# FFN gate and up as seven block products instead of eight in a two-layer hybrid decoder, one core

## The chip, the cores and the metric

The kernel runs on one core of a Trainium2 chip. The metric is the device time of one execution in microseconds (us). TensorE (PE) multiplies, with its weight loads shown apart as PEld; VectorE (DVE) and ScalarE (ACT) do elementwise work; GpSimd (POOL) does the inverse square roots; SyncE (SP) issues the DMAs.

## What is computed

Two layers over 1040 tokens (16 meta tokens and 1024 others), model width 1024, FFN width 2816. Cut to what matters here:

```python
h = h + concat(attn_out, conv_out) @ w_out[l]
hn = rmsnorm(h, norm2_g[l])
gate, up = split(hn @ w_gate_up[l], 2)
h = h + (silu(gate) * up) @ w_down[l]
```

The attention and convolution halves ahead of it, the other norm and the rotary tables are as before in both kernels.

## The kernel before

Activations lie transposed: 128 channels on the partitions, tokens along the free axis, eight such blocks (`acc[n]`) for the residual. Every float32 factor of a matmul is split into a float32r part `hi` (ACT copy) and a rest `lo` (DVE subtraction), and a product is the three passes hi·hi, hi·lo, lo·hi: `mm3` (L248 to L255) with one weight load for each matmul of 128x128 weights by a chunk of tokens. `wsplit` (L195 to L215) loads a weight block in two halves of at most 128x512 into `wr`, and makes `wh` on ACT (L209) and `wl` on DVE (L210). `fetch` (L240) makes a weight one place ahead of its use.

Layer 0 goes over tokens in chunks of 272, 384 and 384 (`CH0`), layer 1 in two of 512 (`CH1`), since the meta tokens are not needed at its end. After attention and convolution come, in each layer:

- the second half of the output projection ("oc", L737 to L748): eight blocks n of 12 matmuls for each chunk, into the `pj` banks of PSUM (three of them); DVE adds each chunk to `acc[n]` (L268), `gsplit` (L263) makes `hh[n]`, `hl[n]` (the FFN's input with the norm's gain), and `accum_sq` (L140) sums the squares;
- `rsqrt_bcast` (L157): sums over partitions by PE, the power on POOL, and a broadcast by 16 or 18 small matmuls with `ones` (L186);
- the FFN (L753 to L804): for each of the 22 blocks j of 128 FFN channels and each chunk, 24 matmuls for gate and 24 for up (contraction 8 x 128, three passes), then DVE and ACT make silu(gate)·up and split it into `mh`, `ml`. After each of four groups (6, 6, 5, 5 blocks in layer 0; 6, 6, 6, 4 in layer 1) the down projection runs: eight blocks n, each chunk 3·(blocks in the group) matmuls, added to `acc[n]`. In the last group each chunk is also split again for the next layer (layer 0) or normed and stored (layer 1, in chunks of 512, 256, 256), and its squares are summed.

The order on each engine is made by the framework's scheduler from the order of the code; each engine works through its own list in order. PSUM has eight banks: `pj` 3, `sc` 3, `tr` 2; the FFN turns through all eight (`PS_ORDER`).

Of the kernel before, what the change touches and what calls it, by code (L numbers as in the profile page):

```python
# [10 lines left out]
F32 = mybir.dt.float32  # L11
# [3 lines left out]
ALU = mybir.AluOpType  # L15
# [15 lines left out]
GROUPS = ((6, 6, 5, 5), (6, 6, 6, 4))  # L31
# [8 lines left out]
WB = 3  # L40
# [5 lines left out]
RB = 4  # L46
SB = 15
PS_BUFS = {"pj": 3, "sc": 3, "tr": 2}
PS_ORDER = ("pj", "tr", "pj", "tr", "pj", "sc", "sc", "sc")
# [4 lines left out]
# columns of the packed per-partition parameters  # L54
# [28 lines left out]
def build(tc, xT, w_in, w_out, w_gu, w_down, params, lams, ctab, consts, tabs, outT):  # L83
# [31 lines left out]
    def tmp(dt=F32):  # L115
        return tp.tile([P, 512], dt, tag="T", name=nm("T"), bufs=TB)
# [40 lines left out]
    def rsqrt_bcast(sq, n, blocks=range(NQ), out=None, cols=False):  # L157
        """[128, tokens] sums over partitions -> (sum/n + eps)^-1/2 on every partition."""
# [36 lines left out]
    def wsplit(src, kn, scale=None, where=None):  # L195
        """Load [128, kn, 128] of weights and split it (scaled) into float32r parts."""
        if where is None:
            hi = wp.tile([P, KD * P], F32R, tag="wh", name=nm("wh"), bufs=WB)
            lo = wp.tile([P, KD * P], F32R, tag="wl", name=nm("wl"), bufs=WB)
        else:  # L200
            hi, lo = where[:, :kn * P], where[:, kn * P:2 * kn * P]
        hk = -(-kn // 2)
        for b0, b1 in ((0, hk), (hk, kn)):
            raw = wp.tile([P, 4 * P], F32, tag="wr", name=nm("wr"), bufs=RB)
            rw = raw[:, :(b1 - b0) * P]
            nc.sync.dma_start(rw, src[:, b0:b1, :].rearrange("p k n -> p (k n)"))
            sl = slice(b0 * P, b1 * P)
            if scale is None:
                S.activation(hi[:, sl], rw, AF.Copy)  # L209
                V.tensor_tensor(lo[:, sl], rw, hi[:, sl].bitcast(F32), op=ALU.subtract)  # L210
            else:
                S.activation(hi[:, sl], rw, AF.Copy, scale=scale)
                V.scalar_tensor_tensor(lo[:, sl], rw, scale, hi[:, sl].bitcast(F32),
                                       op0=ALU.mult, op1=ALU.subtract)
        return hi, lo  # L215

    # Weights in the order of their use; each fetch also prepares the next one.
    plan, made = [], {}

    def make_plan(sub_ts):  # L220
        for l in range(DEPTH):
# [4 lines left out]
            for n in range(KD):  # L226
                plan.append((("oc", l, n), (w_out[l, n, :, 4:8, :], 4), False))
            f0 = 0
            for gi, gn in enumerate(GROUPS[l]):
                for j in range(f0, f0 + gn):  # L230
                    for t in range(2):
                        plan.append((("gu", l, j, t), (w_gu[l, j, t], KD), False))
# [7 lines left out]
    def fetch(*key):  # L240
        i = [p[0] for p in plan].index(key)
        while made_n[0] < len(plan) and made_n[0] <= i + AHEAD:
            k, args, own = plan[made_n[0]]
            made[k] = wsplit(*args, where=big(F32R) if own else None)
            made_n[0] += 1
        return made.pop(key)

    def mm3(out, w, xs, c0, c1):  # L248
        """out = sum over k of w[k]^T x[k], each factor in its two float32r parts."""
        wh, wl = w  # L250
        n = len(xs)
        for q, (wt, xi) in enumerate(((wh, 0), (wh, 1), (wl, 0))):
            for k in range(n):
                T_.matmul(out, lhsT=wt[:, k * P:(k + 1) * P], rhs=xs[k][xi][:, c0:c1],  # L254
# [52 lines left out]
    def project_qk(l, h, cosr, sinr, st, pre=None):  # L307
# [3 lines left out]
        else:  # L311
# [85 lines left out]
    def attention(l, h, stacks, v0, vv, nlam, cats, fin):  # L397
        q0 = 1 if l == DEPTH - 1 else 0
        oall = big()
        o0 = tp.tile([META, P], F32, tag="o0", name=nm("o0"), bufs=2)  # L400
# [5 lines left out]
        def scores(i):  # L406
# [3 lines left out]
            for c in range(2):  # L410
# [3 lines left out]
                for k0, k1 in key_chunks(qb):  # L414
# [5 lines left out]
                    if e > k0:  # L420
                        # the maximum of each part lands next to the diagonal block
# [15 lines left out]
        def turn(i, a):  # L437
# [4 lines left out]
            for g, ge in gs:  # L442
                ptg = ps("tr")
                if g == 1:
                    T_.transpose(ptg[:META, 384:384 + sz], a[:sz, 0:META], ident[:sz, :sz])
                    aT0 = tp.tile([META, P], F32, tag="aT0", name=nm("aT0"), bufs=2)
# [4 lines left out]
                aT = tp.tile([P, 512], F32, tag="aT", name=nm("aT"), bufs=3)  # L451
# [63 lines left out]
    def glu(l, j, rs, out):  # L515
        z = big()
        ct = None
        if j not in DVEJ:
            ct = tp.tile([P, 320], F32, tag="ct", name=nm("ct"), bufs=2)
# [26 lines left out]
    def conv_dve(l, j, z, out):  # L546
        """Queue the taps of one channel block as background work on VectorE."""
# [10 lines left out]
    def conv(l, j, z, ct, out):  # L558
# [9 lines left out]
        for g in range(8):  # L568
            w = wp.tile([P, 5 * P], F32, tag="cw", name=nm("cw"), bufs=CB)
# [72 lines left out]
    for l in range(DEPTH):  # L642
        last = l == DEPTH - 1
# [91 lines left out]
        drain(fill)  # L735
        sqacc = big()
        for n in range(KD):  # L737
            w = fetch("oc", l, n)
            for c0, c1 in chunks:
                po = ps("pj")  # L740
                mm3(po[:, :c1 - c0], w, ccats, c0, c1)
                t = acc[n]
                tt(t[:, c0:c1], po[:, :c1 - c0], t[:, c0:c1], ALU.add)
                if n == KD - 1:
                    accum_sq(sqacc, n == 0, t[:, c0:c1], c0, c1)
                gsplit(hh[n][:, c0:c1], hl[n][:, c0:c1], t[:, c0:c1], col("g2", l, n))
                if n < KD - 1:
                    accum_sq(sqacc, n == 0, t[:, c0:c1], c0, c1)  # L748

# [1 line left out]
        rs = rsqrt_bcast(sqacc, D, range(1 if last else 0, NQ))  # L751
        nps[0] = 0
        f0 = 0  # L753
        for gi, gn in enumerate(GROUPS[l]):
            mids = []
            for j in range(f0, f0 + gn):
                wg = fetch("gu", l, j, 0)
                wu = fetch("gu", l, j, 1)
                mh, ml = big(F32R), big(F32R)
                for c0, c1 in chunks:  # L760
                    n = c1 - c0
                    pg, pu = ps("any"), ps("any")
                    mm3(pg[:, :n], wg, hs, c0, c1)
                    mm3(pu[:, :n], wu, hs, c0, c1)
                    t1, t2 = tmp(), tmp()
                    tt(t1[:, :n], pg[:, :n], rs[:, c0:c1], ALU.mult)
                    S.activation(t1[:, :n], t1[:, :n], AF.Silu)  # L767
                    tt(t2[:, :n], pu[:, :n], rs[:, c0:c1], ALU.mult)
                    tt(t2[:, :n], t2[:, :n], t1[:, :n], ALU.mult)
                    split(mh[:, c0:c1], ml[:, c0:c1], t2[:, :n])  # L770
                mids.append((mh, ml))
            end = gi == len(GROUPS[l]) - 1
            if end:
                sqacc = big()
            ws = {}
            if end and last:
                order = [(n, [c]) for c in CHF for n in range(KD)]
                rs = big()
            else:
                order = [(n, chunks) for n in range(KD)]  # L780
            for n, cs in order:
# [4 lines left out]
                for c0, c1 in cs:  # L786
                    po = ps("any")
# [109 lines left out]
```

## Time and profile before

| | |
|---|---|
| median of 3 runs | 2504.01 us (2503.77 to 2506.76) |
| profiled execution, span | 2505.8 us (its time outside the span is not listed apart) |
| PE busy | 2464.8 us (98%), 14140 matmuls |
| PEld busy | 2253.5 us (90%) |
| DVE busy | 1321.0 us (53%) |
| ACT busy | 823.0 us (33%) |
| granted TensorE clock, mean | 0.995 |

A busy PE says that matmuls follow each other, each overlapping the next; how fast they follow is read from the pieces of the chain of waits: its length divided by the count of matmuls in it. "x24" is such a count. In a timeline, "x2" joins instructions that overlap by a little, so the time from one start to the next is shorter than the duration of one.

### The profile page before, as it was taken

What the parts mean: (1) busy time and instruction counts of PE and PEld (TensorE: products, weight loads), DVE (VectorE), ACT (ScalarE), POOL (GpSimd) and SP (SyncE); (2) the same over time, 40 slices, a digit from 0 to 9 for tenths busy, and PEclk for the clock granted to TensorE, in tenths of its full rate; (3) what the DMA queues carried; (4) which work ended last, traced back from release to release, by engine and by line L of the source; (5) the groups of instructions that cost most, each with busy time, mean ns of one, the idle gap of its engine ahead of it and who ended that gap; (6) DMA issues with size and microseconds to landing.
All of it is one profiled execution on the core that took longest, in us unless ns stands there. A gap on an engine that the chain in (4) does not pass through costs nothing.

```text
span 2505.8 us, 35578 instructions
## 1 busy us (share of the span) xinstructions
PE 2464.8 (98%) x14140; PEld 2253.5 (90%) x14140; DVE 1321.0 (53%) x2967; ACT 823.0 (33%) x1816; POOL 31.8 (1%) x21
## 2 busy tenths in 40 slices
PE   7999999999999999999999999999999999999998
PEld 7999999999999999999999999977888888888887
DVE  7676899743333323333556668987333333333336
ACT  5555543622112112112435555436211121121112
POOL 0000000000000000000000000000000000000000
PEclk9999999999999999999999999999999999999999
DMA  4431322111111111111244303221111111111112
GB/s 165 118 77 39 107 60 53 55 50 38 47 57 43 39 55 48 37 59 37 92 121 101 73 30 111 62 49 60 43 45 50 56 41 47 51 49 44 53 33 84
DMA packets 91365, 155.21 MB, mean 62 GB/s; under 512 B 10816, under 2 KB 46656, under 8 KB 91200
## 3 DMA queue, kind: packets, MB, share of 16 engines
q1 hardware_dynamic: 91200, 152.95, 20.8%
q8 instruction: 111, 1.82, 0.3%
q14 instruction: 54, 0.44, 0.1%
HBM read 114.64 MB, written 8.45 MB: 49 GB/s over the span
## 4 chain that ended last, share of the span: by engine, by line
PE 89%; DVE 7%; issue 1%; POOL 1%; ACT 1%; DMA 1%; SPq 0%; POOLq 0%; DVEq 0%; ACTq 0%
PE pj L254 41%; PE sc L254 22%; PE tr L254 15%; PE tr L465 4%; DVE S L552 3%; PE sc L417 1%; PE tr L454 1%; PE sc L418 1%; PE sc L186 1%; DVE S L268 1%; POOL s L174 1%; PE sc L579 1%; PE sc L167 0%; PE sc L598 0%; POOL s L497 0%
## 5 line engine op out<-in xcount | busy, mean ns | idle before, releaser
L209 ACT ACTIVATE wh<-wr 128x512 fp32r<-128x512 f32 (+2 forms) x406 | 213.8, 570 | 504.6 <-PE sc L254 203.3
L254 PE MATMUL pj<-hh,wh 128*128 128x384 f32 (+2 forms) x1552 | 316.2, 339 | 0.7 <-ACT S L330 0.7
L254 PE MATMUL pj<-hl,wh 128*128 128x384 f32 (+2 forms) x1552 | 310.8, 337 | 0.0
L254 PE MATMUL pj<-hh,wl 128*128 128x384 f32 (+2 forms) x1552 | 307.4, 336 | 0.0
L254 PEld LDWEIGHTS pj<-hl,wh 128*128 128x128 f32 x1552 | 259.1, 188 | 12.8 <-issue 0.2
L254 PEld LDWEIGHTS pj<-hh,wl 128*128 128x128 f32 x1552 | 258.5, 189 | 12.8 <-issue 0.2
L254 PEld LDWEIGHTS pj<-hh,wh 128*128 128x128 f32 x1552 | 257.4, 189 | 14.0 <-ACT S L330 1.0
L254 PE MATMUL pj<-S,wh 128*128 128x384 f32 (+2 forms) x1252 | 261.4, 351 | 2.8 <-ACT S L260 1.3
L210 DVE TENSOR_TENSOR wl<-wr,wh 128x512 fp32r<-128x512 f32 (+2 forms) x406 | 239.2, 616 | 10.1 <-ACT wh L209 8.7
L254 PEld LDWEIGHTS pj<-S,wh 128*128 128x128 f32 x1252 | 214.4, 188 | 25.4 <-ACT S L260 2.3
L268 DVE TENSOR_TENSOR T<-pj,S 128x384 f32<-128x384 f32 (+2 forms) x185 | 99.2, 546 | 213.6 <-PE pj L254 208.7
L260 ACT ACTIVATE S<-T 128x384 fp32r<-128x384 f32 (+2 forms) x110 | 60.4, 549 | 393.0 <-DVE T L268 393.0
L268 DVE TENSOR_TENSOR T<-sc,S 128x512 f32<-128x512 f32 (+2 forms) x81 | 47.6, 588 | 240.4 <-PE sc L254 240.4
L552 DVE SCALAR_TENSOR_TENSOR S<-S,par,S 128x1039 f32<-128x1039 f32 (+14 forms) x120 | 153.4, 1278 | 0.5
L767 ACT ACTIVATE T<-T 128x384 f32<-128x384 f32 (+2 forms) x110 | 60.4, 549 | 254.4 <-DVE T L268 254.4
L268 DVE TENSOR_TENSOR T<-tr,S 128x384 f32<-128x384 f32 (+2 forms) x62 | 35.7, 580 | 198.7 <-PE tr L254 198.7
L254 PE MATMUL pj<-S,wl 128*128 128x384 f32 (+2 forms) x626 | 139.1, 349 | 0.0
L254 PE MATMUL sc<-hh,wl 128*128 128x512 f32 (+2 forms) x648 | 134.9, 351 | 0.0
L254 PE MATMUL sc<-hh,wh 128*128 128x512 f32 (+2 forms) x648 | 134.9, 351 | 0.0
L254 PE MATMUL sc<-hl,wh 128*128 128x512 f32 (+2 forms) x648 | 134.7, 350 | 0.0
L254 PE MATMUL sc<-S,wh 128*128 128x384 f32 (+3 forms) x684 | 133.8, 343 | 0.0
L254 PEld LDWEIGHTS sc<-S,wh 128*128 128x128 f32 x684 | 114.9, 188 | 10.3
(156 smaller groups left out, 3695.3 us busy)
## 6 DMA issues: line engine op xcount, KB each, us to landing
wr<-in_w_gu SPq DMA_DIRECT2D x176, 256.0 KB, 2.7
S<-ST SPq DMA_DIRECT2D x96, 260.0 KB, 5.4
wr<-in_w_in SPq DMA_DIRECT2D x80, 256.0 KB, 3.5
wr<-in_w_down SPq DMA_DIRECT2D x96, 192.0 KB, 2.4
wr<-in_w_out SPq DMA_DIRECT2D x64, 128.0 KB, 2.2
S<-in_xT SPq DMA_DIRECT2D x8, 520.0 KB, 6.9
wr<-in_w_down SPq DMA_DIRECT2D x32, 128.0 KB, 2.3
S<-in_tabs SPq DMA_DIRECT2D x4, 520.0 KB, 5.9
```

Source lines behind the costliest of these rows:

```text
L174: G.tensor_tensor(rc[:, i0:i1], ms[:, i0:i1], mhalf[:, i0:i1], op=ALU.pow)
L186: T_.matmul(pb[:, a - k0:b - k0], lhsT=ones[:n_, :], rhs=dg[:n_, a - k0:b - k0], start=True, stop=True)
L209: S.activation(hi[:, sl], rw, AF.Copy)
L210: V.tensor_tensor(lo[:, sl], rw, hi[:, sl].bitcast(F32), op=ALU.subtract)
L254: T_.matmul(out, lhsT=wt[:, k * P:(k + 1) * P], rhs=xs[k][xi][:, c0:c1], start=(q == 0 and k == 0), stop=(q == 2 and k == n - 1))
L260: S.activation(hi, src, AF.Copy)
L268: V.tensor_tensor(o, a, b, op=op)
L417: T_.matmul(pc[:sz, :n], lhsT=qs[:, qa:qb], rhs=kk[:, k0:k1], start=True, stop=False)
L418: T_.matmul(pc[:sz, :n], lhsT=qs[:, qa:qb], rhs=kl[:, k0:k1], start=False, stop=True)
L465: T_.matmul(po[:sz, :P], lhsT=lh, rhs=rh, start=(j == 0), stop=(j == len(blocks) - 1))
L552: bg.append(lambda o=o: V.scalar_tensor_tensor(y[:, o:L], z[:, :L - o], cw(o), y[:, o:L], op0=ALU.mult, op1=ALU.add))
L767: S.activation(t1[:, :n], t1[:, :n], AF.Silu)
```

## The change

The FFN's input is cut into two halves of tokens (520 in layer 0, 512 in layer 1) and two halves of the contraction (blocks k 0 to 3 and 4 to 7); the weights of a block j are gate and up by the same two halves. That is a product of 2x2 blocks, and it is made in seven block products in place of eight. For this

- `forms` makes seven forms of the input, each as hi and lo, for k = 0 to 3, after every second block of the oc projection, whose blocks now come as 0, 4, 1, 5, ... (`OCN`): three `gsplit`, four plain splits and four sums or differences of 520 (512) columns on DVE; the squares are summed there too. They take the 16 tiles of `hh` and `hl` and 12 `S` tiles;
- `prep` makes seven forms of the weights of each block j: four raw 128x512 halves are loaded, four sums or differences on DVE (x, x, y, x), and seven splits;
- `product` runs 12 matmuls for each sub-chunk: two of 260 columns in layer 0, one of 512 in layer 1. Partial sums move between PSUM banks by ACT copies and DVE adds;
- all weights share one ring of 16 tiles of 128x512 (`WB`); tiles of the mixing stage lie in a pool that is closed before the FFN, whose space the FFN's `m` tiles use;
- there are eight FFN groups (six of 3 blocks, two of 2) in each layer, and a group's down projection runs after the second product of the next block; after the last group it runs at once. It uses the `pj` and `sc` banks in turn, of which the products hold two each in layer 0 and one each in layer 1.

```diff
-GROUPS = ((6, 6, 5, 5), (6, 6, 6, 4))
+GROUPS = ((3, 3, 3, 3, 3, 3, 2, 2), (3, 3, 3, 3, 3, 3, 2, 2))
...
+        def forms(k):
+            (a0, a1), (b0, b1) = half
+            x, y = acc[k], acc[k + 4]
+            g, e = col("g2", l, k), col("g2", l, k + 4)
+            stt = lambda o, a, sc, b, op: V.scalar_tensor_tensor(o, a, sc, b, op0=ALU.mult, op1=op)
+            s1, s2, s3, s4, d = [tmp()[:, :H] for _ in range(5)]
+            put("a11", k, x[:, a0:a1], g)
+            S.activation(s4, y[:, b0:b1], AF.Copy, scale=e)
+            stt(s3, x[:, b0:b1], g, s4, ALU.subtract)
+            put("s3", k, s3)
+            tt(d, x[:, b0:b1], x[:, a0:a1], ALU.subtract)
+            stt(s2, d, g, s4, ALU.subtract)
+            put("s2", k, s2)
+            put("a12", k, y[:, a0:a1], e)
+            put("s1", k, d, g)
+            stt(s1, y[:, a0:a1], e, s2, ALU.add)
+            put("a22", k, s1)
+            put("s4", k, s4)
...
+            for c, (s0, s1) in enumerate(sub):
+                for p, (wi, xi) in enumerate(((0, 0), (0, 1), (1, 0))):
+                    for k in range(4):
+                        T_.matmul(outs[c][:, :s1 - s0], lhsT=w[wi][:, k * P:(k + 1) * P],
+                                  rhs=xc[q][k][xi][:, s0:s1], start=(first and p == 0 and k == 0),
+                                  stop=(p == 2 and k == 3), skip_group_check=True)
...
+        for i, n in enumerate(OCN):
             w = fetch("oc", l, n)
...
+            if i % 2:
+                forms(n - 4)
+                squares(n - 4)
+                squares(n)
...
+                if q == "a11":
+                    sa = [ps("pj") for _ in sub]
+                    product(sa, j, q, True)
+                    for c, (s0, s1) in enumerate(sub):
+                        S.activation(sb[c][:, :s1 - s0], sa[c][:, :s1 - s0], AF.Copy)
+                elif q == "s3":
+                    sd = [ps("tr") for _ in sub]
+                    product(sd, j, q, True)
...
+                elif q == "s2":
+                    product(sb, j, q, False)
...
+                elif q == "a12":
+                    product(sa, j, q, False)
...
+                elif q == "s1":
+                    product(sb, j, q, False)
...
+                elif q == "a22":
+                    product(sd, j, q, False)
...
+                else:
+                    product(sb, j, q, False)
```

Two places in the order of the instructions. The first is on DVE in layer 0, in the oc projection. Before, one chunk's add (L268, from a `pj` bank into `acc`), its split (L265) and its square sum (L146) alternate:

```order
L268 TENSOR_TENSOR ST_4402<-pj_5109,ST_4402 128x384
L210 TENSOR_TENSOR wl_5194<-wr_5195,wh_5193 128x256
L210 TENSOR_TENSOR wl_5194<-wr_5199,wh_5193 128x256
L265 SCALAR_TENSOR_TENSOR hl_87<-ST_4402,par,hh_79 128x384
L268 TENSOR_TENSOR ST_4402<-pj_5136,ST_4402 128x272
L265 SCALAR_TENSOR_TENSOR hl_88<-ST_4402,par,hh_80 128x272
L146 TENSOR_TENSOR S_5064<-S_5064,T_5152 128x272
L268 TENSOR_TENSOR ST_4402<-pj_5155,ST_4402 128x384
```

Now (L285 is the add, L777 and L768 are the forms' sums and splits, L158 the square sums), between the last add of the first pair of blocks and the first add of the second pair:

```order
L285 TENSOR_TENSOR p_4443<-pj_5172,p_4443 128x384
L222 TENSOR_TENSOR w_5221<-w_5218,w_5220 128x512
L777 SCALAR_TENSOR_TENSOR T_5188<-ST_4441,par,T_5189 128x520
L285 TENSOR_TENSOR T_5190<-ST_4441 128x520
L768 TENSOR_TENSOR hh_85<-T_5189,hh_85 128x520
...
L768 TENSOR_TENSOR hh_84<-T_5186,hh_84 128x520
L158 TENSOR_TENSOR S_5071<-S_5071,T_5215 128x520
L285 TENSOR_TENSOR ST_4441<-pj_5224,ST_4441 128x272
```

The forms and square sums now stand in one piece of 11 instructions ahead of the next add, which empties a `pj` bank.

The second place is on ACT in the FFN of layer 0. Before, weight copies (L209), silu (L767) and the copies of its result (L260):

```order
L209 ACTIVATE wh_7571<-wr_7573 128x512
L209 ACTIVATE wh_7571<-wr_7577 128x512
L767 ACTIVATE T_7563<-T_7563 128x384
L209 ACTIVATE wh_7581<-wr_7583 128x512
L209 ACTIVATE wh_7581<-wr_7587 128x512
L260 ACTIVATE S_7395<-T_7564 128x384
L767 ACTIVATE T_7643<-T_7643 128x272
```

Now (L277 copies of weights and results, L949 and L965 silu, L932, L938 and L943 copies out of PSUM banks that PE adds to again):

```order
L277 ACTIVATE w_8193<-w_8093 128x512
L943 ACTIVATE T_8125<-sc_5624 128x260
L943 ACTIVATE T_8125<-sc_5625 128x260
L277 ACTIVATE w_8226<-w_8224 128x512
L949 ACTIVATE T_8156<-T_8156 128x520
L277 ACTIVATE w_8266<-w_8263 128x512
L277 ACTIVATE w_8302<-w_8099 128x512
L277 ACTIVATE w_8335<-w_8262 128x512
L277 ACTIVATE m_8014<-T_8156 128x520
L965 ACTIVATE T_8254<-T_8254 128x520
L932 ACTIVATE sc_5624<-pj_8270 128x260
```

Copies on which a later product waits now stand behind copies of weights of the next block (w_8193 is made from a raw tile that a DMA fills).

## Rows read from the trace of the kernel before

**Rows 1.** The page: busy time, share of the span, instructions; then the granted clock.
```profile
PE 2464.8 (98%) x14140; PEld 2253.5 (90%) x14140; DVE 1321.0 (53%) x2967; ACT 823.0 (33%) x1816; POOL 31.8 (1%) x21
...
PEclk9999999999999999999999999999999999999999
```

**Rows 2.** Busy time by stage: length, each engine's busy us, clock, DMA share, GB/s.
```profile
463.00:507.00 44.00, 43.82 (x278) 43.50 (x277) 37.33 (x82) 26.91 (x60) 0.00 (x0) 1.00 0.21 67
507.00:1268.00 761.00, 759.51 (x4793) 758.78 (x4791) 289.39 (x571) 169.70 (x338) 1.79 (x1) 1.00 0.16 52
1705.00:1751.00 46.00, 44.47 (x191) 35.84 (x192) 38.03 (x64) 26.18 (x49) 0.00 (x0) 1.00 0.25 81
1751.00:2444.00 693.00, 691.96 (x3008) 562.80 (x3007) 229.75 (x372) 129.47 (x228) 2.01 (x1) 1.00 0.15 46
2444.00:2506.00 62.00, 50.13 (x323) 44.80 (x321) 41.20 (x97) 17.67 (x42) 2.40 (x3) 0.94 0.25 85
```

**Rows 3.** The chain of waits in order of time: start, length, engine, tile, line, matmuls.
```profile
521.08 4.21 PE pj L254 x24
...
563.78 11.42 PE sc L254 x72
...
1761.48 5.56 PE tr L254 x24
...
2476.86 4.24 PE sc L254 x36
```

**Rows 4.** Timeline, the last down projection of layer 1 in chunks of 256.
```profile
2480.82 1.48 PEld L254 LDWEIGHTS pj<-S,S 128*128 128x128 f32 x12
2480.93 1.58 PE L254 MATMUL pj<-S,S 128*128 128x256 f32 x12
```

**Rows 5.** Timeline of DVE at the end of layer 0 and in the final norm.
```profile
1250.05 0.50 DVE L265 SCALAR_TENSOR_TENSOR hl<-p,par,hh 128x272 fp32r<-128x272 f32 x1 [0.59 <-ACT hh L264]
1250.47 0.43 DVE L146 TENSOR_TENSOR S<-S,T 128x272 f32<-128x272 f32 x1
...
1268.03 0.56 DVE L268 TENSOR_TENSOR p<-tr,p 128x384 f32<-128x384 f32 x1 [0.26 <-PE tr L254]
1268.50 1.28 DVE L210 TENSOR_TENSOR wl<-wr,wh 128x512 fp32r<-128x512 f32 x2
1269.70 0.61 DVE L265 SCALAR_TENSOR_TENSOR hl<-p,par,hh 128x384 fp32r<-128x384 f32 x1
1270.23 0.55 DVE L146 TENSOR_TENSOR S<-S,T 128x384 f32<-128x384 f32 x1
...
2473.34 2.74 DVE L801 SCALAR_TENSOR_TENSOR ST<-ST,par,S 128x512 f32<-128x512 f32 x4 [0.80 <-ACT S L189]
...
2486.83 1.67 DVE L801 SCALAR_TENSOR_TENSOR ST<-ST,par,S 128x256 f32<-128x256 f32 x4 [0.68 <-ACT S L189]
```

**Rows 6.** Groups by line and shape: busy us, mean ns of one, idle before them.
```profile
L268 DVE TENSOR_TENSOR T<-T,T 128x512 f32<-128x512 f32 x44 | 30.3, 689 | 2.5
...
L268 DVE TENSOR_TENSOR T<-pj,S 128x272 f32<-128x272 f32 x50 | 21.1, 437 | 25.5 <-PE pj L254 24.2 <-ACT S L189 1.2
...
L209 ACT ACTIVATE wh<-wr 128x512 fp32r<-128x512 f32 x256 | 148.7, 623 | 263.8 <-PE sc L254 111.6 <-PE pj L254 76.1 <-PE tr L254 66.9
L767 ACT ACTIVATE T<-T 128x512 f32<-128x512 f32 x44 | 27.8, 633 | 124.3 <-DVE T L268 124.3
```

**Rows 7.** Timeline of PE at the two FFN norms: 16 small matmuls after a pause.
```profile
514.85 0.36 PE L186 MATMUL sc<-T,ones 16*128 16x16 f32 x2 [1.49 <-DVE T L185]
...
515.49 3.50 PE L186 MATMUL sc<-T,ones 128*128 128x128 f32 x16
...
1758.51 2.02 PE L186 MATMUL sc<-T,ones 128*128 128x128 f32 x16 [1.04 <-DVE T L185]
```

**Rows 8.** PE busy and granted clock in a stretch after the first pause.
```profile
516.00:518.00 2.00, 2.00 (x11) 0.50 0.00 0
```

**Rows 9.** The page, DMA issues: KB each, median us to landing.
```profile
wr<-in_w_gu SPq DMA_DIRECT2D x176, 256.0 KB, 2.7
```

More of the change, by code (lines that the diff above doesn't have):

```diff
@@ L238, in build, with make @@
     made_n = [0]
-    def fetch(*key):
-        i = [p[0] for p in plan].index(key)
-        while made_n[0] < len(plan) and made_n[0] <= i + AHEAD:
+    def make(i):
+        while made_n[0] <= i:
             k, args, own = plan[made_n[0]]
@@ L735, in build, with put @@
         drain(fill)
+        t0 = chunks[0][0]
+        H = (L - t0) // 2
+        half = ((t0, t0 + H), (t0 + H, L))
+        sub = ((0, H),) if H <= 512 else ((0, H // 2), (H // 2, H))
         sqacc = big()
-        for n in range(KD):
+        homes = hh + hl
+        xc = {q: [None] * 4 for q in PRODS}
+        def put(q, k, src, g=None):
+            t = homes.pop(0) if homes else big(F32R)
+            hi, lo = t[:, 0:H], t[:, TW:TW + H]
+            if g is None:
+                S.activation(hi, src, AF.Copy)
+                V.tensor_tensor(lo, src, hi.bitcast(F32), op=ALU.subtract)
+            else:
+                gsplit(hi, lo, src, g)
+            xc[q][k] = (hi, lo)
@@ new lines, in squares, with load7, hilo @@
+        def squares(n):
+            for c0, c1 in half:
+                accum_sq(sqacc, n == 0, acc[n][:, c0:c1], c0, c1)
+        raws, made7 = {}, {}
+        def load7(j):
+            raws[j] = []
+            for t, h in ((0, 0), (1, 0), (1, 1), (0, 1)):
+                r = slot()
+                nc.sync.dma_start(r, w_gu[l, j, t, :, 4 * h:4 * h + 4, :].rearrange("p k n -> p (k n)"))
+                raws[j].append(r)
+        def hilo(j, q, src):
+            hi, lo = slot(F32R), slot(F32R)
+            split(hi, lo, src)
+            made7[j, q] = (hi, lo)
@@ new lines, in build, with ahead, product @@
+        steps = [(j, q) for j in range(NF) for q in PRODS]
+        nprep = [0]
+        def ahead(i):
+            while nprep[0] < min(len(steps), i + 1):
+                j, q = steps[nprep[0]]
+                prep(j, q)
+                if q == "s1" and j + 1 < NF:
+                    load7(j + 1)
+                nprep[0] += 1
+        def product(outs, j, q, first):
+            w = made7.pop((j, q))
+            for c, (s0, s1) in enumerate(sub):
[4 more added lines that the diff above has]
+                                  stop=(p == 2 and k == 3), skip_group_check=True)
@@ L738, in build @@
+        ahead(1)
+        for i, n in enumerate(OCN):
             w = fetch("oc", l, n)
+            t = acc[n]
             for c0, c1 in chunks:
@@ L741, in build, with down @@
                 mm3(po[:, :c1 - c0], w, ccats, c0, c1)
-                t = acc[n]
                 tt(t[:, c0:c1], po[:, :c1 - c0], t[:, c0:c1], ALU.add)
[L744 to L771, printed above, removed]
+            if i % 2:
+                forms(n - 4)
+                squares(n - 4)
+                squares(n)
+        close_phase()
+        open_phase(f"ffn{l}")
+        sb = [ps("sc") for _ in sub]
+        for c, (s0, s1) in enumerate(sub):
+            T_.matmul(sb[c][:, :s1 - s0], lhsT=xc["a11"][0][0][:, :P], rhs=xc["a11"][0][0][:, s0:s1],
+                      start=True, stop=True)
+        jobs, later, sq = [], [], [None]
+        nd = [0]
+        def down(gi, f0, gn, mids):
             end = gi == len(GROUPS[l]) - 1
+            ws = {}
             if end:
-                sqacc = big()
-            ws = {}
+                sq[0] = big()
             if end and last:
                 order = [(n, [c]) for c in CHF for n in range(KD)]
-                rs = big()
+                rf = big()
             else:
@@ L805, in build @@
+        for f in later:
+            f()
+        for job in jobs:
+            down(*job)
+        sqacc = sq[0]
+        close_phase()
     ctx.close()
```

183 lines of the change are left out of this document (140 added, 43 removed).

## The prediction

> **What bounds the kernel now.** I read the page first: PE is busy 98% of the span at full granted clock, DVE 53% [rows 1]. Then busy time by stage: the two FFN stages, 761 and 693 us, make up over half of the time, and in them PE pauses for less than 2 us each, while DVE is busy a third of the time and the DMA engines 15% [rows 2]. So PE's stream of matmuls sets the time there, and the question is what one matmul costs in it. Busy PE does not tell that, the pieces of the chain do [rows 3]: 24 matmuls of 384 columns take 4.21 us, 175.4 ns each; 24 of 512 take 5.56 us, 231.7 ns; 36 of 256 take 4.24 us, 117.8 ns. A piece of 72 that holds two chunks of 384 and one of 272 takes 11.42 us, which leaves (11.42 - 2 x 4.21)/24 = 125.0 ns for 272. Per column that is 0.453 to 0.460 ns at every width, so time follows the columns, with next to no fixed part. For 260 columns I take 117.8 + 4 x (125.0 - 117.8)/16 = 119.6 ns.
>
> **The products.** Layer 0, one block j. Before: 48 matmuls of each of three chunks, 48 x 125.0 + 96 x 175.4 ns = 22.84 us. Now: 7 products x 2 sub-chunks x 12 = 168 matmuls x 119.6 ns = 20.09 us. Saved: 2.75 us x 22 blocks = 60.5 us. Layer 1: 96 x 231.7 ns = 22.24 us before, 7 x 12 = 84 x 231.7 = 19.46 us now, 2.78 x 22 = 61.2 us saved. All of it is on the path, as PE is what ends last there. From the profiled span: 2505.8 - 60.5 - 61.2 = 2384.1 us. The down projection has the same matmuls as before, in more groups.
>
> **What is put beside the products.** DVE instructions that follow each other start at a shorter pitch than their duration [rows 5]: a 384 add 0.47 us (1268.03 to 1268.50), a 512 subtraction 0.60, a scaled split 0.53 of 384, 0.42 of 272, 0.685 of 512 (2.74/4). For 520 I take 0.61 plain and 0.69 scaled, for 272 plain 0.35 and 260 plain 0.34 (0.437 less the same 0.09 [rows 6]). A block j in layer 0 then costs DVE 11 weight instructions x 0.60 + 8 of 260 x 0.34 + 6 of 520 x 0.61 = 13.0 us of 20.1. ACT has 7 weight copies (0.62), 2 silu and 2 copies (0.63 [rows 6]) and 6 short copies (0.4 or less), some 9 us. Neither becomes the bound. The new waits are the hand-overs in PSUM: each bank that PE adds to again is first copied by ACT or read by DVE, with at least one other product (2.8 us) between. The longest chain is from the last product over silu, two multiplications and a copy on ACT to the copy into `sc`: about 0.6 + 0.7 + 0.7 + 0.7 + 0.65 us, and PE needs it 5.6 us later. I cost the hand-overs at nothing; their cover is the products between. Bounds: 0, and 0.5 us for each of 44 blocks, 22 us. The raw weights are the same bytes as before and land in 2.7 us [rows 9]; they are asked for several products ahead.
>
> **The start of the FFN.** Here the cover is thin already: DVE was busy 37.3 of 44.0 us in the oc projection of layer 0, 38.0 of 46 in layer 1 [rows 2]. A pair of oc blocks now asks DVE for 6 adds (2.6 us), 2 weight halves (1.2), 6 scaled instructions (4.1), 5 plain ones (3.05) and 4 square sums (2.4): 13.4 us against 2 x 12 x (125.0 + 2 x 175.4) ns = 11.4 us of PE. And the forms stand in one piece ahead of the next add, while PE has only three `pj` banks. From the last matmul of a pair: add 0.7, weight half 0.6, ACT's scaled copy 0.65, the piece 7.1, first add 0.35: some 9.5 us, in which PE can fill three banks, 5.7 us. PE waits 3.8 us after the first pair, and 4.5 to 5 after the next two (two square sums more): 13.5 us. In layer 1 three banks are 8.3 us of PE work, so the waits are 1.4, 2.6 and 2.6; with the last forms some 8 us. Bounds: 10 us for both layers if the scheduler's order lets adds slip in, 38 if every piece is 3 us longer through ACT.
>
> **The end of each layer.** In the last group DVE does, for each block of layer 0, adds 1.3 us, splits 0.42 + 2 x 0.53 = 1.5, squares 1.3 and weights 0.35: 4.4 us, 35 us for eight. With 5 blocks in that group PE took 8 x 15 x 0.476 = 57 us, which hid it; with 2 it takes 22.8 us. Add 3 us for the last half's silu chain, less the first squares: DVE ends some 37 us after the last product, so PE loses 14 us. In layer 1 the group shrinks from 4 to 2: PE 22.4 us, DVE 12.3 (chunk of 512) + 2 x 5.3 + norms 5.5 + 2 x 3.4 + chain 2.4 = 37.6. The stage was 62 us with 44.9 of matmuls; now I get some 45, 6 more than 62 less the 22.5 us of matmuls that moved to other groups. Bounds for both: 10 and 32. The other groups of two lose perhaps 2 us on the two free banks in layer 0.
>
> **The clock.** After a pause of 1.49 us the granted clock was 0.50 [rows 7, 8], and 16 small matmuls took 3.50 us, where after one of 1.04 us they took 2.02 [rows 7]. So a long pause can cost 1.5 us more. With three pauses at the start of layer 0 and one at its end: 4 x 1.5 = 6 us. Bounds 0 and 12.
>
> **The sum.** 2384.1 + 13.5 + 8 + 14 + 6 + 2 + 6 = 2433.6 us of span. The median of the runs lies 1.8 us under the profiled span, so 2432 us, 2.9% less than 2504.01. With the low bounds it is 2384.1 + 10 + 10 - 1.8 = 2402; with the high ones 2384.1 + 38 + 32 + 12 + 22 + 4 - 1.8 = 2490. The mixing stages only change the ring of their weights; I cost them at nothing (what hides it: weights one place ahead), with 4 us either way.
>
> **The rivals.**
>
> *The ends are hidden.* DVE's pieces could be interleaved with the adds, and the next layer's first matmuls with the last splits. For it: DVE has slack over each stage as a whole, and blocks of `hh` are ready one by one. Against it: the order shows the piece in one, and the first product of the next layer asks for all eight blocks. Time: about 2395 us (2384.1 + 13 - 1.8).
>
> *Every block loses a little.* Hand-overs in two short sub-chunks, or a bank read late since an ACT copy waits behind another engine, cost 0.7 us a block. For it: the new ACT order mixes three kinds of waits in one list. Against it: at least 1 us of slack in the chain above. Time: 2432 + 44 x 0.7 = 2463 us.
>
> *Late weights, slower.* In ACT's new order a copy that PE waits for stands behind the copy of the next block's first raw weights. If the shared ring frees those tiles only when the last product has used them, each block waits for a load (2.7 us [rows 9]) and a copy (0.62), less what is covered: some 3 us, 44 x 3 = 132 us, 2564 us. It turns slower than before from (2504 - 2432)/44 = 1.6 us a block. Against it: the ring has 16 tiles and a block's live ones are some 13 when the loads are placed.
>
> *Weight loads as the bound, slower.* In layer 0's FFN the weight loads too are busy 758.8 of 761 us, 4791 of them, 158 ns each [rows 2]; if that were the time a load needs, 168 loads in place of 144 would take 26.6 us a block: 83 us lost in layer 0 where I have 60.5 saved, 2575 us. Against it: 12 loads took 1.48 us beside matmuls of 256 columns [rows 4], 123 ns each, so a load shortens with its matmul. This is the rule of the Trainium skill, Perfetto Trace Analysis, section Identifying the Most-Contended Engine: headroom on TensorE is judged by the busy share of LDWEIGHTS, not of matmuls. By that rule layer 0 has no headroom in loads and the change adds loads; the row for 256 columns speaks for the columns, so I give the rule a small chance.
>
> **How the numbers follow.** Forecast 0.61; ends hidden 0.15; a little in every block 0.17; late weights 0.05; load bound 0.02. The time is the forecast's, 2432 us. The range 2398 to 2478 takes in most of the first two rivals and the bounds, and leaves out the two slow cases and the ends of the others. A measurement of this kernel tells 0.2% (5 us) from no change. Slower: the two slow cases, less a little, 0.06; within 0.2%: 0.02 from between; faster: 0.92.
>
> **What would show it.** Right: products of 12 matmuls in 1.44 us (260) or 2.78 us (512) that follow each other without idle time of PE inside the FFN; PE waiting on DVE in the oc projection, some 4 us at a time, and at the end of layer 0; DVE near full there. Wrong: PE waiting on ACT copies in every block; ACT waiting on raw weight loads; 260 columns at over 125 ns; the oc stage no longer than before.

## The result and the profile after

The changed kernel takes **2446.45 us** (median of 4 runs, 2446.08 to 2447.56) against 2505.26 us for the kernel before in the same runs: a ratio of 0.9764 (95% interval 0.9750 to 0.9778). The forecast was 2432 us, the range 2398 to 2478. The profiled execution took 2446.08 us, its span is 2444.3 us. The page of after, to be set beside [rows 1]:

```profile
PE 2369.1 (97%) x14359; PEld 2154.2 (88%) x14359; DVE 1689.7 (69%) x3532; ACT 991.1 (41%) x2090; POOL 32.4 (1%) x21
...
PEclk9999999999999999999989999999999999999998
```

PE is busy 95.7 us less, the span is only 61.5 us shorter: PE's idle time grew by 34 us. DVE went from 53% to 69%. The products themselves came out as forecast. The chain of waits in the two FFN stages (start, length, engine, tile, line, matmuls):

```profile
553.50 2.87 PE sc L856 x24
...
573.62 2.86 PE sc L856 x24
...
1769.03 2.78 PE pj L856 x12
```

24 matmuls of 260 columns take 2.87 us, 119.6 ns each; a block of layer 0 takes 573.62 - 553.50 = 20.12 us (forecast 20.09), a product of layer 1 2.78 us. So the products lose nothing. To place the loss, the span is cut at four instructions that both kernels have: the small norm matmul ahead of each oc projection, and the first matmul of each last down projection. On PE's timeline before:

```profile
439.92 0.39 PE L186 MATMUL sc<-T,ones 16*128 16x16 f32 x2 [1.30 <-DVE T L185]
...
1211.08 1.42 PE L254 MATMUL pj<-S,wh 128*128 128x272 f32 x10
...
1686.81 0.39 PE L186 MATMUL sc<-T,ones 16*128 16x16 f32 x2 [1.03 <-DVE T L185]
...
2444.33 2.92 PE L254 MATMUL pj<-S,S 128*128 128x512 f32 x12
```

and after:

```profile
444.79 0.39 PE L198 MATMUL sc<-T,ones 16*128 16x16 f32 x2 [1.00 <-DVE T L197]
...
1208.72 0.29 PE L271 MATMUL pj<-S,w 128*128 128x272 f32 x1
...
1662.73 0.39 PE L198 MATMUL sc<-T,ones 16*128 16x16 f32 x2 [1.16 <-DVE T L197]
...
2391.70 0.39 PE L271 MATMUL pj<-S,S 128*128 128x512 f32 x1
```

"Due" is the length before, less what the products save (60.5 us in layer 0, 61.2 in layer 1), with the down matmuls moved that now belong to an earlier group: 3 blocks in layer 0 (72 x (125.0 + 2 x 175.4) ns = 34.3 us), 2 in layer 1 (96 x 231.7 ns = 22.2 us).

| stretch | before | after | due | lost | forecast |
|---|---|---|---|---|---|
| mixing of layer 0, to the norm | 439.9 | 444.8 | 439.9 | 4.9 | 0 |
| oc and FFN of layer 0, to the last product | 771.2 | 763.9 | 744.9 | 19.0 | 13.5 + 2 + 4.5 = 20 |
| last down of layer 0, mixing of layer 1 | 475.7 | 454.0 | 441.5 | 12.5 | 14 + 1.5 = 15.5 |
| oc and FFN of layer 1, to the last product | 757.5 | 729.0 | 718.5 | 10.5 | 8 |
| final stage | 61.5 | 52.6 | 39.2 | 13.4 | 6 |
| sum | 2505.8 | 2444.3 | 2384.1 | 60.2 | 49.5 |

Two profiles of one stage differ as well: the mixing of layer 0 takes 442.8 to 446.8 us in seven traces that share it with the changed kernel, and 439.9 and 440.1 in two that share it with the kernel before.

Busy time in stretches of after (length; PE, PEld, DVE, ACT, POOL; granted clock, DMA share, GB/s): mixing of layer 0 after its first pause, oc of layer 0, a stretch within it, its FFN, the end of layer 0, FFN of layer 1, final stage:

```profile
70.00:81.00 11.00, 9.96 (x40) 8.52 (x40) 6.09 (x31) 4.23 (x17) 0.00 (x0) 0.53 0.26 86
467.30:530.30 63.00, 51.53 (x299) 50.68 (x298) 49.66 (x84) 28.62 (x49) 0.00 (x0) 0.92 0.10 30
504.40:511.00 6.60, 6.60 (x26) 6.60 (x27) 3.77 (x8) 1.25 (x2) 0.00 (x0) 0.55 0.00 0
540.00:1208.72 668.72, 666.90 (x5089) 665.23 (x5088) 417.83 (x782) 218.32 (x427) 2.18 (x1) 1.00 0.17 50
1238.00:1254.00 16.00, 14.75 (x59) 14.05 (x60) 9.31 (x23) 5.03 (x11) 2.25 (x1) 0.50 0.63 219
1760.00:2391.70 631.70, 631.70 (x2727) 511.77 (x2727) 389.49 (x612) 204.87 (x354) 0.00 (x0) 1.00 0.17 52
2391.70:2444.30 52.60, 31.68 (x177) 27.57 (x175) 38.14 (x90) 13.89 (x34) 2.40 (x3) 0.79 0.23 80
```

In these stretches of the FFN PE has no idle time at all in layer 1, and 1.8 us in layer 0. At the edges PE is idle, and afterwards, though busy, it works for a while at the lower of its two clock levels (0.50, 1.2 GHz): the granted clock is 0.53, 0.55 and 0.50 in the stretches of 11.0, 6.6 and 16.0 us above. PE's timeline at the edges (in brackets the idle time before and what ended it):

```profile
488.30 11.61 PE L271 MATMUL pj<-S,w 128*128 128x272 f32 x72 [2.93 <-DVE ST L285]
...
504.36 15.83 PE L271 MATMUL pj<-S,w 128*128 128x272 f32 x84 [4.21 <-DVE ST L285]
...
524.50 5.80 PE L271 MATMUL pj<-S,w 128*128 128x384 f32 x24 [4.07 <-DVE ST L285]
...
1235.67 0.39 PE L271 MATMUL sc<-S,w 128*128 128x272 f32 x1 [1.79 <-DVE w L222]
...
1239.25 3.84 PE L271 MATMUL pj<-hh,w 128*128 128x272 f32 x12 [2.37 <-ACT w L221]
...
2421.22 1.01 PE L179 MATMUL sc<-ones,S 128*128 128x1 f32 x4 [3.91 <-DVE S L158]
```

The first three are the forecast waits for an add that stands behind a piece of forms. The last three belong to the ends of the layers.

### The profile page after: what moved, and what is told of

It is laid out like the page before. It is cut to its first block, busy times and chain, and to the rows that moved or that the text cites. A ratio compares the mean times of both kernels' runs of the same rounds, so it can differ in the third digit from the quotient of the medians.

```text
span 2444.3 us, 36772 instructions
## 1 busy us (share of the span) xinstructions
PE 2369.1 (97%) x14359; PEld 2154.2 (88%) x14359; DVE 1689.7 (69%) x3532; ACT 991.1 (41%) x2090; POOL 32.4 (1%) x21
## 4 chain that ended last, share of the span: by engine, by line
PE 82%; DVE 12%; ACT 2%; issue 1%; POOL 1%; DMA 1%; SPq 1%; DVEq 0%; POOLq 0%; ACTq 0%
PE pj L271 25%; PE sc L856 15%; PE pj L856 10%; PE tr L856 10%; PE sc L271 9%; PE tr L482 4%; DVE S L569 3%; PE sc L434 2%; PE tr L471 1%; PE sc L435 1%; DVE S L158 1%; PE sc L198 1%; DVE T L285 1%; DVE S L285 1%; PE sc L179 1%
## 5 line engine op out<-in xcount | busy, mean ns | idle before, releaser
L271 PE MATMUL pj<-S,w 128*128 128x384 f32 (+2 forms) x1425 | 358.2, 357 | 16.9 <-DVE ST L285 13.4
L271 PE MATMUL pj<-hh,w 128*128 128x384 f32 (+1 forms) x1776 | 348.5, 331 | 3.1 <-ACT w L221 2.4
L277 ACT ACTIVATE w<-w 128x512 fp32r<-128x512 f32 x308 | 187.2, 627 | 309.8 <-DVE w L285 129.5
L271 PEld LDWEIGHTS pj<-hh,w 128*128 128x128 f32 x1776 | 290.6, 192 | 6.0 <-ACT w L221 2.7
L271 PEld LDWEIGHTS pj<-S,w 128*128 128x128 f32 x1425 | 254.6, 192 | 45.6 <-DVE ST L285 15.2
L856 PE MATMUL sc<-S,w 128*128 128x260 f32 (+1 forms) x1188 | 283.9, 320 | 0.0
L278 DVE TENSOR_TENSOR w<-w,w 128x512 fp32r<-128x512 f32 x308 | 210.1, 688 | 95.5 <-ACT w L277 35.9
L271 PE MATMUL sc<-m,w 128*128 128x384 f32 (+3 forms) x834 | 229.8, 349 | 0.0
L271 PE MATMUL pj<-m,w 128*128 128x384 f32 (+3 forms) x825 | 226.9, 349 | 0.0
L856 PEld LDWEIGHTS sc<-S,w 128*128 128x128 f32 x1188 | 196.3, 188 | 17.4
L222 DVE TENSOR_TENSOR w<-w,w 128x512 fp32r<-128x512 f32 (+2 forms) x219 | 130.9, 598 | 92.4 <-ACT w L221 47.0
L856 PE MATMUL sc<-hh,w 128*128 128x260 f32 (+1 forms) x594 | 189.8, 320 | 0.7 <-ACT sc L932 0.7
```

Of the source, the lines that this page charges most:

```text
L222: V.tensor_tensor(lo, rw, hi.bitcast(F32), op=ALU.subtract)
L271: T_.matmul(out, lhsT=w[k][wi], rhs=xs[k][xi][:, c0:c1], start=(q == 0 and k == 0), stop=(q == 2 and k == n - 1))
L277: S.activation(hi, src, AF.Copy)
L278: V.tensor_tensor(lo, src, hi.bitcast(F32), op=ALU.subtract)
L856: T_.matmul(outs[c][:, :s1 - s0], lhsT=w[wi][:, k * P:(k + 1) * P], rhs=xc[q][k][xi][:, s0:s1], start=(first and p == 0 and k == 0), stop= ...
```

## The experiments

All of them are edits of the changed kernel but the first. "Less" and "more" are against its median, 2446.45 us. The kernel before, run again beside each series, had medians of 2504.6 to 2507.2 us, so a difference of 2 us between series says nothing. The edits are cut to the lines that matter.

**1. The groups alone, in the kernel before.**

```diff
-GROUPS = ((6, 6, 5, 5), (6, 6, 6, 4))
+GROUPS = ((3, 3, 3, 3, 3, 3, 2, 2), (3, 3, 3, 3, 3, 3, 2, 2))
```

> The kernel before with only the eight smaller FFN groups of the change (last group of 2 in both layers); its products stay eight. Theory (the ends of the layers lose time because the last down projection is too short to hide DVE's norm work): the stretch from the last down projection of layer 0 to the next layer loses some 10 us, the final stage some 10 us, so about 2525 us (2515 to 2535). Rival (small groups are free, the losses of the changed kernel's ends come from its products, forms and shared weight ring): 2505 us, within 4.

Measured: 2528.46 us, 1.0098 of the kernel before (1.0082 to 1.0114), some 24 us slower. By the cut of the table the end of layer 0 loses 11.6 us and the final stage 11.3, without any of the new products; the other three stretches lose 0.2, 0.0 and 1.1. PE's timeline in the final stage shows the waits for the square sums of the second and the last chunk, which were none and 1.82 us with a group of 4:

```profile
2509.09 1.01 PE L167 MATMUL sc<-ones,S 128*128 128x1 f32 x4 [5.84 <-DVE S L146]
...
2519.23 0.94 PE L167 MATMUL sc<-ones,S 128*128 128x1 f32 x4 [2.89 <-DVE S L146]
```

**2. Three blocks in the last group.**

```diff
-GROUPS = ((3, 3, 3, 3, 3, 3, 2, 2), (3, 3, 3, 3, 3, 3, 2, 2))
+GROUPS = ((2, 2, 3, 3, 3, 3, 3, 3), (2, 2, 3, 3, 3, 3, 3, 3))
```

> The changed kernel with the two groups of 2 first and six of 3 after, so that the last down projection of each layer has 3 blocks (34 us of matmuls in place of 23). Theory (DVE's 36 us at each end is fixed, and PE waits for what of it is not covered): layer 0's end loses 8 us less and the final stage 8 to 10 us less, 2429 us (2424 to 2435). Rival (the end's loss is late weights behind the saves on SP's queue and has nothing to do with the group's size): 2446 us, within 4.

Measured: 2427.03 us, 0.9689 of the kernel before (0.9672 to 0.9706), 19.4 us less. The end of layer 0 by stretch:

```profile
1190.00:1245.00 55.00, 54.98 (x383) 54.59 (x382) 45.07 (x96) 29.96 (x65) 1.06 (x1) 1.00 0.40 140
```

34 us of matmuls, from 1202.77 on, cover DVE's chain: no idle time and no fall of the clock up to 1245, and then one wait of 1.1 us for the norm. By the cut of the table the end of layer 0 now takes 451.9 us and loses nothing (452.9 due with 3 blocks); the final stage takes 56.4 and loses 6.1 (50.3 due).

**3. The forms cut into steps.** Each step has one DVE instruction; `PER`, the steps behind each add, is (3, 4) for the two layers.

```diff
+                for _ in range(PER[l]):
+                    if pend:
+                        pend.pop(0)()
             if i % 2:
-                forms(n - 4)
-                squares(n - 4)
-                squares(n)
+                pend += forms_steps(n - 4) + square_steps(n - 4) + square_steps(n)
+        for f in pend:
+            f()
```

> The changed kernel with the forms and square sums of a pair of blocks cut into single steps that are put behind the adds of the next pair (three steps behind each add in layer 0, four in layer 1). Theory (PE waits because the piece of 11 DVE instructions stands as one ahead of the next add, with three pj banks): the waits of 2.9, 4.2 and 4.1 us in the oc projection of layer 0 shrink to under 2 us each and the clock there falls less; 8 us less in layer 0, 2 in layer 1, 2436 us (2432 to 2441). Rival (DVE's total work bounds the stage, the order does not matter, the waits only move to the norm of the first block): 2446 us, within 4.

Measured: 2436.22 us, 0.9729 (0.9714 to 0.9745), 10.2 us less. By the cut of the table oc and FFN of layer 0 take 9.2 us less (754.8), those of layer 1 no less at all (729.1, 729.0 without the edit). In the oc projection of layer 0 the three waits for an add behind the forms are gone, and a part of the rival is true as well: some of the loss moved into the first FFN block, where PE now waits for the last pair's forms and for the norm. In layer 1 the outcome is the whole of the rival's: nothing is won. PE in layer 0:

```profile
515.94 0.39 PE L867 MATMUL pj<-S,w 128*128 128x260 f32 x1 [1.41 <-DVE S L283]
...
530.99 2.15 PE L199 MATMUL sc<-T,ones 16*128 16x16 f32 x8 [1.85 <-DVE T L198]
```

**4. The first head's stacks on POOL's queue** (`first` is true for head 0 of layer 0). First the queue of SP in the changed kernel: the loads of the next head's weights (L215) stand behind twelve copies of stacks (L378) that wait for their source, and the next loads are issued at 66.34.

```profile
52.41 0.43 SPq L215 DMA_DIRECT2D w<-in_w_in  x1
53.05 13.19 SPq L378 DMA_DIRECT2D S<-ST  x12
66.34 3.66 SPq L215 DMA_DIRECT2D w<-in_w_in  x4
```

```diff
-                    nc.sync.dma_start(s[64 * j:64 * j + 64, :L].bitcast(F32), st[x][rows].bitcast(F32))
+                    (nc.gpsimd if first else nc.sync).dma_start(s[64 * j:64 * j + 64, :L].bitcast(F32), st[x][rows].bitcast(F32))
```

> The changed kernel with the 12 copies of the first head's stacks (layer 0) issued on POOL's queue, which is idle, in place of SP's. Theory (in the mixing stage's start the weight loads of the next head stand on SP behind these copies, PE runs out of work for 3.6 us and then works at the lower clock for 11 us): 5 us less, 2441 us (2439 to 2443). Rival (the loads wait for free tiles of the shared weight ring, not for the queue): 2446 us, within 2.

Measured: 2439.55 us, 0.9737 (0.9722 to 0.9753), 6.9 us less; the mixing of layer 0 takes 438.8 us in place of 444.8. The loads are issued from 54.32 on. PE still waits 1.58 us for a stack, but the clock stays:

```profile
65.00:81.00 16.00, 15.01 (x91) 14.51 (x92) 9.67 (x31) 6.03 (x21) 0.92 (x2) 1.00 0.70 165
```

**5. The saves at the end of layer 0 on POOL's queue.**

```diff
-                    nc.sync.dma_start(hsave[n], t)
+                    nc.gpsimd.dma_start(hsave[n], t)
```

> The changed kernel with the eight saves of the residual at the end of layer 0 issued on POOL's queue in place of SP's, groups as in the change. Theory (there the last weights of the down projection and the first of layer 1 stand on SP behind saves that wait for DVE's adds; PE waits 1.8 and 2.4 us for their copies and then works at the lower clock for 17 us): 6 us less, 2440 us (2435 to 2443). Rival (the copies are late because ACT and DVE are busy with the norm, not because the loads are late): 2446 us, within 3.

Measured: 2445.0 us (median of 3 runs, 2443.06 to 2448.44), 0.9764 (0.9748 to 0.9780): nothing. The theory falls. SP now asks for layer 1's weights at 1218.19, 15 us sooner, and PE's two waits are the same:

```profile
1237.87 0.40 PE L271 MATMUL sc<-S,w 128*128 128x272 f32 x1 [1.78 <-DVE w L222]
...
1241.45 3.83 PE L271 MATMUL pj<-hh,w 128*128 128x272 f32 x12 [2.37 <-ACT w L221]
```

The releaser's name (a weight's copy on ACT or DVE) had hidden the cause: those copies stand in their engines' order behind the adds, splits and squares of the norm, and DVE is busy in this run for all of the 20 us from 1224 to 1244.

**6. Useless matmuls in the pauses of the oc projection of layer 0.**

```diff
+NFILL = 24
...
             if i % 2:
                 forms(n - 4)
                 squares(n - 4)
                 squares(n)
+                if i < 7 and l == 0:
+                    fb = ps("sc")
+                    for _ in range(NFILL):
+                        x = xc["s2"][n - 4][0]
+                        T_.matmul(fb[:, :256], lhsT=x[:, :P], rhs=x[:, :256], start=True, stop=True)
```

> The changed kernel with 24 extra matmuls of 256 columns (2.8 us of PE) after each of the first three pairs of the oc projection of layer 0, into a spare bank that nobody reads; they wait for the s2 form, so they fall into the pause in which PE waits for the add. Theory (of the 18 us lost before the end of the FFN some 5 are not the waits but the lower clock after them): the waits' sum stays, the clock does not fall at 504 and 524 us, 2442 us (2440 to 2445). Rival (the extra matmuls only delay PE, or the lower clock costs nothing there): 2446 us or more.

Measured: 2435.66 us, 0.9729 (0.9712 to 0.9745), 10.8 us less, with 72 matmuls more. The oc projection by stretch:

```profile
467.00:524.00 57.00, 55.36 (x363) 54.02 (x362) 48.28 (x84) 28.33 (x48) 0.00 (x0) 1.00 0.08 26
```

and on PE's timeline what is left of the wait of 4.2 us behind 24 of the added matmuls:

```profile
498.29 3.14 PE L877 MATMUL sc<-hl 128*128 128x256 f32 x24
...
502.97 12.23 PE L272 MATMUL pj<-S,w 128*128 128x272 f32 x77 [1.12 <-DVE ST L286]
```

From the norm ahead of oc to the FFN norm the trace takes 90.7 us, 5.0 less than the changed kernel's 95.6, as expected. Only these 5.0 us can be put down to the added matmuls. Five other traces with the same three waits there take 95.2 to 98.6 us, so the 5.0 are known to some 2 us. 4.2 us more come from the stretch after it, at whose end two like waits (1.79 and 2.10 us) were here followed by 8 us of a lower clock, not 17. Why, no run shows; the rest lies in stages that the edit does not touch.

**7. Useless matmuls at the end of layer 0.**

```diff
                 if end and not last:
                     nc.sync.dma_start(hsave[n], t)
+                if end and not last and n >= 6:
+                    fb = ps("tr")
+                    x = hh[n - 1]
+                    a0 = chunks[-1][0] if n == 6 else 0
+                    for _ in range(14 if n == 6 else 18):
+                        T_.matmul(fb[:, :256], lhsT=x[:, a0:a0 + P], rhs=x[:, a0:a0 + 256], start=True, stop=True)
```

> The changed kernel with 14 and 18 extra matmuls of 256 columns (1.65 and 2.1 us of PE) at the end of layer 0, into a spare bank that nobody reads, where PE waits 1.8 us for the last low weights and 2.4 us for the first copy of layer 1. Theory (of the 13.6 us lost from the last product of layer 0 to layer 1's oc projection only some 5 are waits and 9 the lower clock that follows them for 18 us): the lower clock goes, the waits stay, 2437 us (2434 to 2441). Rival (PE waits for DVE's 36 us chain in this stretch anyway, so a faster clock only waits longer): 2446 us, within 3.

Measured: 2444.56 us (2442.22 to 2448.51), 0.9752 (0.9735 to 0.9770), 1.9 us less, within the scatter of its runs: the rival is right. The clock did stay up for the most part (0.91; 0.54 in the same stretch of the changed kernel), but from the last product to the first norm of layer 1 only 2.7 us were won:

```profile
1236.00:1254.00 18.00, 15.88 (x101) 14.45 (x100) 13.74 (x33) 7.79 (x17) 2.25 (x1) 0.91 0.72 249
```

PE, now faster, only waits sooner for DVE and for the norm. The lower clock had next to no price of its own there.

**8. A smaller weight ring.**

```diff
-WB = 16
+WB = 13
```

> The changed kernel with 13 tiles in the weight ring in place of 16. Theory (the hand-over of weights cost nothing because three tiles more than a block's live ones let the loads run ahead): PE now waits for weight copies in the FFN blocks, 1 us or more in each of 44, 2490 us or more. Rival (the ring is far from its limit in the FFN): only the mixing stages lose a little, 2446 to 2456 us.

Measured: 2445.66 us (2 runs), 0.9765 (0.9745 to 0.9784). My theory falls again: with three tiles fewer PE still does not wait once for a weight in the FFN (both stages by stretch).

```profile
548.00:1205.00 657.00, 656.95 (x5006) 655.73 (x5007) 410.46 (x767) 217.95 (x422) 0.00 (x0) 1.00 0.16 50
1765.00:2385.00 620.00, 620.00 (x2677) 503.14 (x2676) 381.87 (x598) 201.87 (x345) 0.00 (x0) 1.00 0.17 53
```

What feels the ring is the mixing of layer 0, 6.0 us more up to its norm, and layer 1: in its oc projection PE waits 1.49 and 2.75 us for the rest of a weight from DVE (L222), and oc and FFN take 4.0 us more. In between, from the first of these norms to the FFN norm and from there to the first norm of layer 1, the trace is 4.0 and 5.3 us shorter; at the end of layer 0 the lower clock lasts some 6 us where it was 17. That the sum is nothing is a balance, not a proof that the ring is free.

**9. One norm chain less in the final stage.**

```diff
-CHF = ((16, 528), (528, 784), (784, 1040))
+CHF = ((16, 528), (528, 1040))
```

> The changed kernel with the last down projection of layer 1 in two chunks of 512 columns in place of 512, 256 and 256. Theory (the final stage lost 13 us in place of the 6 forecast because each chunk's norm is a chain over PE, DVE, POOL, DVE, PE, ACT and DVE of 5 us or more, and 22 us of matmuls no longer cover three of them): one chain less, 2441 us (2438 to 2445). Rival (DVE's total of adds, squares and scaling bounds the stage, and a last chunk twice as long has more of it after the last matmul): 2446 us or more.

Measured: 2441.11 us, 0.9732 (0.9712 to 0.9753), 5.3 us less. The final stage takes 47.8 us, 4.8 less, and that is not the chain alone: DVE works 35.5 us in 65 instructions where it was 38.1 in 90, so 2.6 us come from fewer and longer instructions and 2.2 from less idle time of DVE. PE's waits of the last norm:

```profile
2425.19 1.87 PE L179 MATMUL sc<-ones,S 128*128 128x1 f32 x8 [5.71 <-DVE S L158]
...
2428.78 2.08 PE L198 MATMUL sc<-T,ones 128*128 128x128 f32 x8 [1.73 <-DVE T L197]
```

**10. Edits 2, 3 and 4 together.**

> The changed kernel with the three edits that each gave time: groups of 2 first, form steps behind the adds, the first head's stack copies on POOL's queue. Theory (they act in different stages: 19.4, 10.2 and 6.9 us): the gains add up, 2446.5 - 36.5 = 2410 us (2405 to 2416). Rival (the gains share the same recovered clock or move the waits to the first block's norm): 2420 us or more.

Measured: 2412.33 us, 0.9630 (0.9616 to 0.9644), 34.1 us less of 36.5: they add up.

**11. With edit 9 as well.**

> The changed kernel with groups of 2 first, form steps behind the adds, the first head's stack copies on POOL's queue, and the last down projection of layer 1 in two chunks of 512 columns. Theory (the exposed norm chain of the third chunk is worth 5 us where a group of 2 ends layer 1, less where 3 blocks cover more of it): 2 to 4 us below the three edits together, 2409 us (2406 to 2412). Rival (with 3 blocks the third chain is covered already and the longer last chunk costs 2 us): 2414 us.

Measured: 2408.28 us (median of 5 runs, 2408.09 to 2410.20), 0.9618 (0.9606 to 0.9631) of the kernel before, 38.2 us under the change as made. It is the fastest here, and beats both kernels.

## Why the prediction held, and where it was off

**The products** (121.7 us) were right to a tenth of a microsecond per block: time goes with columns (119.6 ns for 260 of them, 231.7 for 512), and the hand-overs in PSUM cost nothing, as their cover said. The rival of 0.7 us in each block is out: PE's idle time in the two FFN stretches shown is 1.8 us in all. Late weights are out too, and by more than I thought: even the ring of 13 did not bring them into the FFN blocks.

**Weight loads as the bound** is out. In layer 0's FFN 5088 loads are busy 665.2 of 668.7 us, 131 ns each, where 4791 were busy 158 ns each [rows 2], while a block took 2.7 us less. The Trainium skill, Perfetto Trace Analysis, section Identifying the Most-Contended Engine, judges TensorE's headroom by the busy share of weight loads, beside the share of peak arithmetic. Read by the loads alone that left no headroom, and adding loads should have cost time; here the measurement decides: a load's busy time shrank with the matmul beside it, so its share told nothing of a limit.

**The start of the FFN**, layer 0: 3.8 and twice 4.5 to 5 us forecast; 2.93, 4.21 and 4.07 measured, for the reason named (experiment 3). The clock, 4.5 us forecast there, gave back 5.0 when the pauses were filled, but that the two agree is luck: the sum takes 1.5 us after each of three pauses, while after the first the clock stayed at 1.00 (488.30 to 499.90), so the other two cost more. In layer 1 the mechanism was wrong for the most part. It lost 10.5 us, 8 forecast, of which the waits for an add were to be 6.6; they are 0.34 us at 1704.08 and these two:

```profile
1717.51 15.72 PE L271 MATMUL pj<-S,w 128*128 128x512 f32 x60 [1.83 <-DVE ST L285]
...
1734.54 0.72 PE L856 MATMUL pj<-hh,w 128*128 128x512 f32 x2 [1.07 <-DVE ST L285]
```

That is 3.2 us, and taking them away won nothing there (experiment 3). What the 10.5 us consist of stays open.

**The end of layer 0**: 15.5 us forecast, 12.5 measured; the smaller groups alone lost 11.6 there (experiment 1). DVE's 37 us were right: on its timeline the last square sum ends 36 us after the last product (1208.72), and PE's column sums take 5 us more.

```profile
1244.34 0.55 DVE L158 TENSOR_TENSOR S<-S,T 128x384 f32<-128x384 f32 x1
...
1250.63 0.17 DVE L182 TENSOR_SCALAR s<-sc 128x8 f32<-128x8 f32 x1 [5.00 <-PE sc L179]
```

Experiments 1 and 2 show that the length of the last group decides, 5 and 7 that neither the loads nor the clock does.

**The final stage** is the term that was mis-sized most: "some 45, 6 more" came out at 52.6, 13.4 more. DVE's work was about right (37.6 forecast, with 2.4 of a chain in it; 38.14 busy). The step that failed is the norms in that sum, "norms 5.5 + 2 x 3.4": by [rows 5] these are the scalings, 2 x 2.74 and 2 x 1.67 us of DVE, and they came out as such. But a norm is a chain over several engines, in which DVE too is idle, and the chain ahead of each scaling has no term in the sum; nor is it said what leads from 37.6 to "some 45". DVE is idle for 14.5 us of the 52.6. 9.2 us of it are waits inside the three chains (in total, times, longest):

```profile
DVE ST L914 <- ACT S L201: 3.4, 3, 1.5
DVE s L182 <- PE sc L179: 3.2, 3, 1.1
DVE T L197 <- POOL s L186: 2.6, 3, 0.9
```

The timeline of the second chunk's, from the last square sum on:

```profile
2419.69 1.48 DVE L158 TENSOR_TENSOR S<-S,T 128x256 f32<-128x256 f32 x3
...
2422.27 0.16 DVE L182 TENSOR_SCALAR s<-sc 128x2 f32<-128x2 f32 x1 [1.10 <-PE sc L179]
...
2422.57 0.70 POOL L186 TENSOR_TENSOR s<-s,mhalf 128x2 f32<-128x2 f32 x1 [14.06 <-DVE s L175]
2423.30 0.48 DVE L197 TENSOR_SCALAR T<-con,s 128x128 f32<-128x128 f32 x2 [0.85 <-POOL s L186]
...
2423.65 1.22 PE L198 MATMUL sc<-T,ones 128*128 128x128 f32 x4 [1.42 <-DVE T L197]
...
2424.90 0.38 ACT L201 ACTIVATE S<-sc 128x256 f32<-128x256 f32 x1 [6.27 <-PE sc L198]
...
2425.32 1.67 DVE L914 SCALAR_TENSOR_TENSOR ST<-ST,par,S 128x256 f32<-128x256 f32 x4 [1.53 <-ACT S L201]
```

With PE's column sums (at 2421.22, above), six steps of 0.2 to 1.2 us take 4.1 us, up to the first scaling. Before, DVE waited 7.0 us in the three chains too, but the next chunk's matmuls covered two of them, and PE ended later; with 22 us less of matmuls they lie open. With the old products the smaller groups lost 11.3 us in this stage (experiment 1). One chain less gave 5.3 us, about half of it through less DVE work (experiment 9), so what a chain costs by itself is not shown closer than that.

**The mixing stages**, "I cost them at nothing (what hides it: weights one place ahead), with 4 us either way", lost 4.9 us in layer 0 (some 2 us either way, by the traces that share it). The total of tiles is that of before, but raw and split weights now share one ring, and 9 loads of `in` weights are issued ahead of the first stack copies on SP's queue where it was 12; that the ring is the reason is argued, not shown. PE waited 1.4 and 2.2 us for stacks with no other matmul to run, then worked 11 us at a granted clock of 0.53. Experiment 4 gave the loss back.

These two terms, 12.3 us, and 2.5 us more in layer 1, less 4 where the forecast was too high, are the 10.7 us between the forecast span (2433.6) and the measured one. The time lies 14.5 us over the forecast; the rest, some 4 us, is the step from span to time, which took 1.8 us off: the profiled run of before was one of the slower, that of after was not, and the median after lies 2.1 us above the span.

## What to carry to other kernels

Where PE never waits, matmuls saved come out of the time in full; the price of such a change is at the stage's edges, where work of other engines loses the matmuls that covered it. So before shrinking the last group of a stage, set the matmuls that are left against the other engine's whole chain, and count a norm as a chain over several engines, not as its instructions. A wait's releaser can be the last step of such a chain: move what feeds that step alone and the wait stays (experiment 5).

## What I had not expected of the hardware

72 matmuls whose result nobody reads made the kernel 10.8 us faster, though only some 5 of these are put down to them: PE kept its full clock through three pauses, of which two had lowered it. 32 more at the end of layer 0 kept it up for the most part and won next to nothing (1.9 us, within the scatter). In these two places the lower clock cost time only where PE was what ended last. And the stretch at the lower clock is no fixed price: after two like waits at the end of layer 0 it was some 17 us in one kernel, 8 in another and 6 in a third. Nor does the length of a pause tell by itself whether it comes: after 2.93 us (488.30) the clock stayed at 1.00 here, while it fell to 0.50 after 1.49 us in the kernel before [rows 7, 8].
